# Fourier branch of a diffusion block: one set of channel sums for both mirrored halves, and SiLU as one activation

## The chip, the cores and the metric

One core of a Trainium2 chip runs the whole block. The metric is the device time of one execution in microseconds (us). The program has five engines that work side by side, each through its own instructions in order: TensorE (PE in the profile, with its weight loads as PEld), VectorE (DVE), ScalarE (ACT), GpSimd (POOL) and SyncE (SP, which here only issues transfers).

## The reference, cut to what matters

The block takes 512 tokens of 2048 channels, projects them, and runs two mixers beside each other: attention, and a Fourier mixer over 512 of the projected channels in four groups of 128. The change lies in the Fourier mixer.

```python
def _fourier_mix(u):                      # u: 1 x 512 x 512
    ug = u.astype(jnp.float32).reshape(b, n, N_FNET_GROUPS, FNET_GROUP)
    y = jnp.fft.fftn(ug, axes=(1, 3), norm="ortho").real
    return y.reshape(b, n, FNET_W).astype(u.dtype)

y_b = (_fourier_mix(u_b) * jax.nn.silu(z_b)) @ w_pb
```

For each group, the real part of a 2-D transform over 512 tokens and 128 channels is wanted. With the token sums A (cosine) and B (sine) at frequency f, and the cosine and sine tables C and S over channels, the output is C·A − S·B. A is even in f and B is odd, so at the mirrored frequency 512 − f it is C·A + S·B. The factor of norm="ortho" is 1/256.

## The kernel before, in words

Every product of float32 data is made as three products of a high and a low half (`mm3`, lines 336 to 340): high by high, high by low, low by high. `split_from` (lines 179 to 181) makes the halves: ScalarE rounds the high half (line 180), VectorE subtracts it to get the low half (line 181). So each 1024-column piece of weights costs one instruction on each of those two engines before TensorE can use it (`whi` and `wlo`, or `s` where the halves lie in other slots).

The program starts with the projections of the Fourier branch, then has a short Fourier stage (lines 893 to 968), then goes through the large groups of weights. The Fourier stage works on four groups g:

- `tokens(g)` (line 918) sums over tokens. It makes 12 products on TensorE into two PSUM banks (`pb`), one for even frequencies (258 columns: 129 cosine, 129 sine) and one for odd ones (256 columns). Each bank is split into `ah` and `al`, with even and odd frequencies interleaved.
- `positions(g)` (line 931) sums over channels. It makes 12 products of 256 columns into one bank (`pd`): the lower 256 frequencies from C·A and −S·B (`t` picks a block of `fch`, which holds C, −S and S), and the mirrored 256 from C·A and S·B again, reading `ah` and `al` backwards. The eight products with `ah` come first (line 939), the four with `al` last (line 942). Line 944 on VectorE multiplies the bank by 1/256 and by the gate held in `part`.
- `gate_b(g)` (line 946) turns z into silu(z): ScalarE takes the sigmoid into `e` (line 949), VectorE multiplies (line 950).

The order of calls is tokens 0 and 1, then for each g: gate, positions, the next tokens, and the splits of the first weight pieces of the following product (line 961). TensorE keeps this written order (line 907). On VectorE and ScalarE a scheduler sets the order when the program is built, so a change in one place can move instructions elsewhere.

Behind the stage come the seven products of the first weight group: P1, Q5, P2, Q6, P7, Q3 and Q4, each of four weight pieces. A piece is 12 matmuls of 512 columns. Their results lie in PSUM tiles called `x`, `y` and later `banks`. Some products need sums of the activations (`S`, `Z`, and `ev`, lines 993 and 994), which VectorE makes and splits as well. Weights come in through buffers `wr` and `R`; line 268 adds two pieces, line 276 subtracts them. `qr` and its lines 1208 to 1216 are the norm and rotation of the attention heads. Line 1182 takes sigmoids of the merge gates much later.

Of the kernel before, what the change touches and what calls it, by code (L numbers as in the profile page):

```python
# [10 lines left out]
F32 = mybir.dt.float32  # L11
F32R = mybir.dt.float32r
ACT = mybir.ActivationFunctionType
ALU = mybir.AluOpType
# [4 lines left out]
P = 128  # L19
D = 2048  # L20
T = 512
# [23 lines left out]
RAW = 4  # L45

HL, MORE_HL = 3, 2
EVEN = 258

# [73 lines left out]
def block_kernel(ctx, tc, xT, ctx_rows, ctx_toks, x, c_row, w_ss, w_gate, vecs, qkg, rope, dft_c, dft_s,  # L123
                 w_start, w_g, w_pab, w_o, final_g, out):
    nc = tc.nc
# [30 lines left out]
    def uid(s):  # L156
        cnt[0] += 1
        return f"{s}{cnt[0]}"
# [20 lines left out]
    def split_from(src, hi, lo):  # L179
        first = nc.scalar.activation(hi, src, ACT.Copy)  # L180
        return first, nc.vector.tensor_tensor(lo, src, hi.bitcast(F32), op=ALU.subtract)  # L181
# [16 lines left out]
    def stream(key, src, *a, **k):  # L198
        todo.append(Piece(key, src if isinstance(src, list) else [src], *a, **k))
# [136 lines left out]
    def mm3(o, ah, al, bh, bl, start, stop, cont=False):  # L336

        nc.tensor.matmul(o, ah, bh, start=start, stop=False, skip_group_check=cont)  # L338
        nc.tensor.matmul(o, ah, bl, start=False, stop=False, skip_group_check=cont)  # L339
        nc.tensor.matmul(o, al, bh, start=False, stop=stop, skip_group_check=cont)  # L340
# [25 lines left out]

    for p in start_pieces():
        if p[2:5:2] == (KK - 4, 0):
            stream(("dfts", 0), dft_s[:, : 2 * EVEN], 2 * EVEN, 2, "raw")
            stream(("dftc", 0), dft_c, 3 * P, 1, "raw")  # L370
        elif p[2:5:2] == (KK - 4, 4):
            stream(("dfts", 1), dft_s[:, 2 * EVEN :], T, 2, "raw")
# [71 lines left out]
    q = NGATE  # L444
# [19 lines left out]
    pst, ppool = region("part", "right")  # L464
    part = ppool.tile([P, NS, T], F32, name="part")
# [47 lines left out]
    with tc.issue_after(nc.scalar.activation(ce, cvt, ACT.Exp, scale=-1.0).ins):  # L513
# [6 lines left out]
    fch = ppool.tile([P, 2, 3 * P], F32R, name="fch")  # L520
    fsq = [ppool.tile([P, 2, 2, EVEN], F32R, name="fsq0")]
    rx = pap.tile([P, T], F32, name="rx")
    wacc = bank3()
    def warm(n, src):
# [203 lines left out]
    def split_table(q):  # L728
        split_from(get(("dfts", q)).rearrange("p (a n) -> p a n", a=2), fsq[q][:, 0], fsq[q][:, 1])
# [46 lines left out]
    with tc.manual_schedule(engines={E.PE}):  # L776
# [6 lines left out]
        with tc.manual_schedule(engines={E.Activation, E.DVE}):  # L783
# [25 lines left out]
            for kb in range(1, 4):  # L809
                k = kb + 1  # L810
# [32 lines left out]
            for kb in range(4, KK - 4, 2):  # L843
# [6 lines left out]
                k = kb + 2  # L850
# [45 lines left out]
    fsq.append(fnp.tile([P, 2, 2, 256], F32R, name="fsq1"))  # L896
    split_table(1)

    def halves(a):
# [16 lines left out]
    AH, low = {}, {}  # L916

    def tokens(g):

        ah, al = (fnp.tile([P, 2, 257], F32R, tag=n, bufs=2, name=uid(n)) for n in ("ah", "al"))  # L920
        c = slice(P * g, P * g + P)
        for e in range(2):
            n = fsq[e].shape[-1]
            acc = bank()
            for a in range(2):
                mm3(acc[:, :n], uh[:, a, e, c], ul[:, a, e, c], fsq[e][:, 0, a, :], fsq[e][:, 1, a, :], a == 0, a == 1)
            k = slice(e, 257 - e, 2)
            low[g] = split_from(acc[:, :n].rearrange("p (r f) -> p r f", r=2), ah[:, :, k], al[:, :, k])[1]
        AH[g] = ah, al

    def positions(g):

        ah, al = AH.pop(g)
        acc = bank2()
        steps = [(256 * q, P * (r and 1 + q), (slice(0, 256) if q == 0 else slice(256, 0, -1)), r)
                 for q in range(2) for r in range(2)]
        for n, (o, t, k, r) in enumerate(steps):
            for m, i in enumerate((0, 1)):
                nc.tensor.matmul(acc[:, o : o + 256], fch[:, i, t : t + P], ah[:, r, k], start=n == m == 0, stop=False,
                                 skip_group_check=True)  # L940
        for n, (o, t, k, r) in enumerate(steps):
            nc.tensor.matmul(acc[:, o : o + 256], fch[:, 0, t : t + P], al[:, r, k], start=False, stop=n == 3,
                             skip_group_check=True)
        nc.vector.scalar_tensor_tensor(part[:, 4 + g, :], acc, 1.0 / 256.0, part[:, 4 + g, :], op0=ALU.mult, op1=ALU.mult)

    def gate_b(g):
        z = part[:, 4 + g, :]
        e = fnp.tile([P, T], F32, tag="sil", bufs=1, name=uid("e"))
        nc.scalar.activation(e, z, ACT.Sigmoid)
        nc.vector.tensor_tensor(z, z, e, op=ALU.mult)  # L950

    tokens(0)
    tokens(1)
# [724 lines left out]
    for i in range(NSTEP + 3):  # L1678
        h, t = divmod(i, 4)
# [20 lines left out]
        n = next((n for n, at in enumerate(SUM_AT) if at <= i < at + 3), None)  # L1700
# [19 lines left out]
        if i in GATE_STEPS:  # L1720
            n = NGATE + GATE_STEPS.index(i)
# [91 lines left out]
    o = {}  # L1813
# [255 lines left out]
```

## Time and profile before

| what | us |
|---|---|
| median of three runs | 1290.94 (1290.84 to 1290.96) |
| the profiled execution | 1290.61 |
| its span, first to last instruction | 1288.8 |
| TensorE busy | 1272.9 |
| VectorE busy | 994.7 |
| ScalarE busy | 682.2 |
| GpSimd busy | 170.8 |

The profiled execution's own time is 1.8 us above its span. A timeline row gives the start in us from the span's start, the time of the instruction (or of several alike, with their count), engine, line, operation, output and inputs. What ended an idle time ahead of it stands in brackets. Neighbouring instructions on one engine overlap a little, so the cost of one in a full queue is the distance from its start to the next start, which is called its pitch here.

### The profile page before, as it was taken

The page shows a single profiled execution, that of the slowest core. Times are in us where ns is not written, and L with a number is a line of the kernel's source. Part 1 is how long each engine was busy: PE and PEld are TensorE (multiplying, and loading weights), DVE is VectorE, ACT ScalarE, POOL GpSimd, SP SyncE. Part 2 cuts the span into 40 slices and gives each one's busy share as a digit, 9 for nine tenths or more (in the row PEclk, how much of TensorE's full clock was granted, in tenths as well). Part 3 has the DMA queues.
Part 4 walks back from the last instruction along what each step waited for, and adds up shares of the span by engine and source line. Part 5 has one row for each costly group of instructions (what it writes and reads, how often), then busy time and mean ns, then how long its engine had stood idle before and what let it go on. Part 6 is the DMA issues. An engine that isn't in the chain of part 4 may idle for free.

```text
span 1288.8 us, 17680 instructions
## 1 busy us (share of the span) xinstructions
PE 1272.9 (99%) x6586; PEld 1047.9 (81%) x6586; DVE 994.7 (77%) x1305; ACT 682.2 (53%) x1073; POOL 170.8 (13%) x222
## 2 busy tenths in 40 slices
PE   8999999999999999999999999999999999999997
PEld 5677887888888888888888888888888888888886
DVE  5767899889779787658587666788898777887677
ACT  5322654645556555444355544666667646464544
POOL 0000011111102011012031010012100211211210
PEclk9999999999999999999999999999999999999999
DMA  9998588888988988977879897578852989998986
GB/s 378 408 369 344 208 216 248 237 218 261 227 302 236 301 269 260 291 197 184 278 207 259 286 249 237 182 245 241 270 178 75 249 244 258 244 211 229 225 200 179
DMA packets 104486, 319.14 MB, mean 248 GB/s; under 512 B 9904, under 2 KB 33072, under 8 KB 100432
## 3 DMA queue, kind: packets, MB, share of 16 engines
q1 hardware_dynamic: 55056, 197.40, 42.3%
q0 software_dynamic: 27024, 98.19, 35.6%
q10 hardware_dynamic: 22320, 22.42, 5.1%
q8 instruction: 51, 0.84, 0.3%
q14 instruction: 35, 0.29, 0.1%
HBM read 283.36 MB, written 34.61 MB: 247 GB/s over the span
## 4 chain that ended last, share of the span: by engine, by line
PE 91%; DVE 3%; DMA 2%; ACT 2%; issue 1%; SPq 0%; ACTq 0%; DVEq 0%
PE banks L338 10%; PE banks L339 10%; PE banks L340 10%; PE x L340 9%; PE x L338 9%; PE x L339 9%; PE y L340 7%; PE y L339 7%; PE y L338 7%; PE banks L1543 2%; PE pd L566 2%; PE pb L338 1%; PE pb L339 1%; PE pb L340 1%; PE pc L338 1%; DMA wa<-in_w_ss 1%
## 5 line engine op out<-in xcount | busy, mean ns | idle before, releaser
L180 ACT ACTIVATE whi<-R 128x1024 fp32r<-128x1024 f32 x138 | 145.6, 1060 | 142.1 <-PE banks L340 55.3
L181 DVE TENSOR_TENSOR wlo<-R,whi 128x1024 fp32r<-128x1024 f32 x138 | 167.9, 1222 | 57.9 <-ACT whi L180 57.6
L181 DVE TENSOR_TENSOR wlo<-wr,whi 128x1024 fp32r<-128x1024 f32 (+1 forms) x122 | 147.2, 1214 | 63.1 <-ACT whi L180 63.1
L180 ACT ACTIVATE whi<-wr 128x1024 fp32r<-128x1024 f32 (+1 forms) x122 | 127.4, 1052 | 127.3 <-PE y L340 44.3
L338 PE MATMUL banks<-whi,s 128*128 128x512 f32 (+1 forms) x400 | 157.8, 394 | 0.9 <-DVE ev L1106 0.9
L339 PE MATMUL banks<-wlo,s 128*128 128x512 f32 (+1 forms) x400 | 155.8, 389 | 0.0
L340 PE MATMUL banks<-whi,s 128*128 128x512 f32 (+1 forms) x400 | 155.8, 389 | 0.0
L338 PE MATMUL x<-whi,s 128*128 128x512 f32 x352 | 137.1, 390 | 0.0
L340 PE MATMUL x<-whi,s 128*128 128x512 f32 x352 | 137.0, 389 | 0.0
L339 PE MATMUL x<-wlo,s 128*128 128x512 f32 x352 | 136.9, 389 | 0.0
L338 PE MATMUL y<-whi,s 128*128 128x512 f32 x316 | 123.1, 389 | 0.2 <-DVE cxe L1266 0.2
L339 PE MATMUL y<-wlo,s 128*128 128x512 f32 x316 | 123.1, 390 | 0.0
L340 PE MATMUL y<-whi,s 128*128 128x512 f32 x316 | 122.8, 389 | 0.0
L291 POOL DMA_DIRECT2D R<-in_w_g x64 | 56.0, 875 | 415.2 <-DVE wlo L181 212.6
L180 ACT ACTIVATE s<-wr 128x512 fp32r<-128x512 f32 (+2 forms) x93 | 60.9, 678 | 68.1 <-DMA wr<-cf_d 24.9
L338 PEld LDWEIGHTS banks<-whi,s 128*128 128x128 f32 x400 | 75.2, 188 | 16.6 <-DVE ev L1106 1.3
L181 DVE TENSOR_TENSOR s<-wr,s 128x512 fp32r<-128x512 f32 (+2 forms) x93 | 66.7, 750 | 28.3 <-ACT s L180 27.5
L340 PEld LDWEIGHTS banks<-whi,s 128*128 128x128 f32 x400 | 75.1, 188 | 15.3
L339 PEld LDWEIGHTS banks<-wlo,s 128*128 128x128 f32 x400 | 75.2, 188 | 13.6 <-DVE wlo L181 0.2
L340 PEld LDWEIGHTS x<-whi,s 128*128 128x128 f32 x352 | 66.1, 188 | 13.8
L339 PEld LDWEIGHTS x<-wlo,s 128*128 128x128 f32 x352 | 66.1, 188 | 13.7
L338 PEld LDWEIGHTS x<-whi,s 128*128 128x128 f32 x352 | 66.1, 188 | 13.6
(322 smaller groups left out, 2803.2 us busy)
## 6 DMA issues: line engine op xcount, KB each, us to landing
wr<-in_w_g SPq DMA_DIRECT2D x128, 512.0 KB, 5.8
R<-in_w_g POOLq DMA_DIRECT2D x64, 512.0 KB, 7.3
wa<-in_w_ss SPq DMA_DIRECT2D x31, 1024.0 KB, 9.7
R<-in_w_g SPq DMA_DIRECT2D x32, 512.0 KB, 6.0
wr<-in_w_gate SPq DMA_DIRECT2D x32, 512.0 KB, 5.1
wr<-in_w_o SPq DMA_DIRECT2D x24, 512.0 KB, 7.5
R<-in_w_o POOLq DMA_DIRECT2D x24, 512.0 KB, 9.2
wr<-in_w_pab SPq DMA_DIRECT2D x20, 512.0 KB, 6.0
```

What stands on the lines that cost most here:

```text
L180: first = nc.scalar.activation(hi, src, ACT.Copy)
L181: return first, nc.vector.tensor_tensor(lo, src, hi.bitcast(F32), op=ALU.subtract)
L291: nc.gpsimd.dma_start(chain[e.pc], e.nxt, accum_op=ALU.add)
L338: nc.tensor.matmul(o, ah, bh, start=start, stop=False, skip_group_check=cont)
L339: nc.tensor.matmul(o, ah, bl, start=False, stop=False, skip_group_check=cont)
L340: nc.tensor.matmul(o, al, bh, start=False, stop=stop, skip_group_check=cont)
L566: nc.tensor.matmul(acc[32 * j : 32 * j + 32], c2[:, n, :], w[:, k, :], start=n < 4, stop=n >= KK - 4)
L1543: nc.tensor.transpose(tp[:, k * P : (k + 1) * P], p[:, k * P : (k + 1) * P], ident)
```

## The change

The channel stage makes C·A and S·B once, each as one `mm3` of 258 columns, into two banks (`pd` and `pc`). ScalarE copies the sine bank to `odd` in SBUF. VectorE joins them: a subtraction for 257 frequencies (line 940 of the changed kernel), an addition for the 255 mirrored ones, which reads both inputs backwards (line 941), and a multiplication by the gate (line 942). The factor 1/256 goes into the table `dft_c`, which loses its −S block. Both frequency halves get 129 columns each, so that `ah` and `al` hold 258. The gate is one SiLU activation on ScalarE, in place.

```diff
-        ah, al = (fnp.tile([P, 2, 257], F32R, tag=n, bufs=2, name=uid(n)) for n in ("ah", "al"))
+        ah, al = (fnp.tile([P, 2, FREQ], F32R, tag=n, bufs=2, name=uid(n)) for n in ("ah", "al"))
...
-            k = slice(e, 257 - e, 2)
+            k = slice(e, FREQ, 2)
...
-        acc = bank2()
-        steps = [(256 * q, P * (r and 1 + q), (slice(0, 256) if q == 0 else slice(256, 0, -1)), r)
-                 for q in range(2) for r in range(2)]
-        for n, (o, t, k, r) in enumerate(steps):
-            for m, i in enumerate((0, 1)):
-                nc.tensor.matmul(acc[:, o : o + 256], fch[:, i, t : t + P], ah[:, r, k], start=n == m == 0, stop=False,
-                                 skip_group_check=True)
-        for n, (o, t, k, r) in enumerate(steps):
-            nc.tensor.matmul(acc[:, o : o + 256], fch[:, 0, t : t + P], al[:, r, k], start=False, stop=n == 3,
-                             skip_group_check=True)
-        nc.vector.scalar_tensor_tensor(part[:, 4 + g, :], acc, 1.0 / 256.0, part[:, 4 + g, :], op0=ALU.mult, op1=ALU.mult)
+        acc = [b()[:, :FREQ] for b in (bank2, bank3)]
+        for r, o in enumerate(acc):
+            t = slice(P * r, P * r + P)
+            mm3(o, fch[:, 0, t], fch[:, 1, t], ah[:, r, :], al[:, r, :], True, True)
+        z = part[:, 4 + g, :]
+        y, odd = (fnp.tile([P, n], F32, tag=t, bufs=2, name=uid(t)) for t, n in (("y", T), ("odd", FREQ)))
+        nc.scalar.copy(odd, acc[1])
+        nc.vector.tensor_tensor(y[:, :257], acc[0][:, :257], odd[:, :257], op=ALU.subtract)
+        nc.vector.tensor_tensor(y[:, 257:], acc[0][:, 255:0:-1], odd[:, 255:0:-1], op=ALU.add)
+        nc.vector.tensor_tensor(z, y, z, op=ALU.mult)
...
-        e = fnp.tile([P, T], F32, tag="sil", bufs=1, name=uid("e"))
-        nc.scalar.activation(e, z, ACT.Sigmoid)
-        nc.vector.tensor_tensor(z, z, e, op=ALU.mult)
+        nc.scalar.activation(z, z, ACT.Silu)
...
-    dft_c = np.concatenate([np.cos(a), -np.sin(a), np.sin(a)], axis=1).astype(np.float32)
+    dft_c = (np.concatenate([np.cos(a), np.sin(a)], axis=1) / 256.0).astype(np.float32)
...
-    dft_s = np.concatenate([table(np.arange(0, T // 2 + 1, 2)), table(np.arange(1, T // 2, 2))], axis=1)
+    dft_s = np.concatenate([table(np.arange(e, FREQ, 2)) for e in range(2)], axis=1)
```

The built programs show what stands where. VectorE at the start of the Fourier stage, before: `part` is the gate's storage, `al` the low halves of the token sums (numbers 1440 and 1460 are groups 0 and 1, 1497 is group 2), `wlo` the low half of a weight piece.

```order
L659 TENSOR_TENSOR part<-pc_1425,part 128x512
L950 TENSOR_TENSOR part<-part,e_1516 128x512
L181 TENSOR_TENSOR al_1440<-pb_1441,ah_1439 128x2x129
L181 TENSOR_TENSOR al_1440<-pb_1450,ah_1439 128x2x128
L950 TENSOR_TENSOR part<-part,e_1557 128x512
L181 TENSOR_TENSOR al_1460<-pb_1461,ah_1459 128x2x129
L181 TENSOR_TENSOR al_1460<-pb_1470,ah_1459 128x2x128
L181 TENSOR_TENSOR wlo_1554<-R_1339,whi_1553 128x1024
L944 SCALAR_TENSOR_TENSOR part<-pd_1482,part 128x512
L181 TENSOR_TENSOR al_1497<-pb_1498,ah_1496 128x2x129
L950 TENSOR_TENSOR part<-part,e_1578 128x512
```

VectorE at the same place in the changed program (line numbers there are 4 lower behind the change, and tile numbers differ a little):

```order
L659 TENSOR_TENSOR part<-pc_1425,part 128x512
L181 TENSOR_TENSOR al_1440<-pb_1441,ah_1439 128x258
L181 TENSOR_TENSOR al_1440<-pb_1450,ah_1439 128x258
L181 TENSOR_TENSOR al_1460<-pb_1461,ah_1459 128x258
L181 TENSOR_TENSOR al_1460<-pb_1470,ah_1459 128x258
L181 TENSOR_TENSOR wlo_1550<-R_1339,whi_1549 128x1024
L940 TENSOR_TENSOR y_1488<-pd_1480,odd_1489 128x257
L941 TENSOR_TENSOR y_1488<-pd_1480,odd_1489 128x255
L181 TENSOR_TENSOR al_1495<-pb_1496,ah_1494 128x258
L942 TENSOR_TENSOR part<-y_1488,part 128x512
```

The gate's multiplications no longer stand between the four `al` rows, and line 944's one row is now three. Further on, the second and third `wlo` of the stage stand behind more of the new rows, and other rows change places up to a `wlo` some 60 rows later; from there the order is the old one.

ScalarE at the same place, before: `ah` are the high halves, line 949 the sigmoid, `whi` the high half of a weight piece.

```order
L180 ACTIVATE whi_1595<-R_1341 128x1024
L180 ACTIVATE ah_1439<-pb_1441 128x2x129
L180 ACTIVATE ah_1439<-pb_1450 128x2x128
L949 ACTIVATE e_1557<-part 128x512
L180 ACTIVATE ah_1459<-pb_1461 128x2x129
L180 ACTIVATE ah_1459<-pb_1470 128x2x128
L949 ACTIVATE e_1578<-part 128x512
```

ScalarE there in the changed program, with the SiLU on line 946 and the copy of the sine bank on line 939:

```order
L946 ACTIVATE part<-part 128x512
L180 ACTIVATE whi_1587<-R_1341 128x1024
L180 ACTIVATE ah_1439<-pb_1441 128x258
L946 ACTIVATE part<-part 128x512
L180 ACTIVATE ah_1439<-pb_1450 128x258
L180 ACTIVATE ah_1459<-pb_1461 128x258
L180 ACTIVATE ah_1459<-pb_1470 128x258
L180 ACTIVATE s_286<-wr_1640 128x2x256
L939 COPY odd_1489<-pc_1481 128x258
```

The third gate has moved ahead of `whi`, and the fourth now stands between the two halves of `ah` of group 0.

ScalarE at the first sigmoid of the merge gates, far behind the stage, before:

```order
L180 ACTIVATE s_433<-R_1342 128x2x256
L180 ACTIVATE s_571<-wr_3569 128x2x256
L1182 ACTIVATE ev_3623<-x_3382 128x1024
L180 ACTIVATE s_734<-wr_3569 128x2x256
L1183 DMA g_d<-ev_3623 128x1024
L180 ACTIVATE whi_3670<-wr_3587 128x1024
```

And in the changed program:

```order
L180 ACTIVATE s_433<-R_1342 128x2x256
L180 ACTIVATE s_571<-wr_3561 128x2x256
L1178 ACT_TABLE_LOAD
L1178 ACTIVATE ev_3615<-x_3374 128x1024
L180 ACTIVATE s_734<-wr_3561 128x2x256
L1179 DMA g_d<-ev_3615 128x1024
L180 ACTIVATE whi_3662<-wr_3579 128x1024
```

One more load of ScalarE's function table stands ahead of that sigmoid.

More of the change, by code (lines that the diff above doesn't have):

```diff
@@ L47 @@
 HL, MORE_HL = 3, 2
-EVEN = 258
+FREQ = 258
 FORMS = ("Z5", "S2", "S3", "S4")
@@ L368, in block_kernel @@
         if p[2:5:2] == (KK - 4, 0):
-            stream(("dfts", 0), dft_s[:, : 2 * EVEN], 2 * EVEN, 2, "raw")
-            stream(("dftc", 0), dft_c, 3 * P, 1, "raw")
+            stream(("dfts", 0), dft_s[:, : 2 * FREQ], 2 * FREQ, 2, "raw")
+            stream(("dftc", 0), dft_c, 2 * P, 1, "raw")
         elif p[2:5:2] == (KK - 4, 4):
-            stream(("dfts", 1), dft_s[:, 2 * EVEN :], T, 2, "raw")
+            stream(("dfts", 1), dft_s[:, 2 * FREQ :], 2 * FREQ, 2, "raw")
         stream(("start", p), w_start[p[0] : p[0] + P * p[1]].rearrange("(p c) -> p c", p=P), p[1], p[2 + 1])
@@ L519, in block_kernel @@
                             ce.rearrange("p (j k) -> p j k", j=2), op=ALU.mult)
-    fch = ppool.tile([P, 2, 3 * P], F32R, name="fch")
-    fsq = [ppool.tile([P, 2, 2, EVEN], F32R, name="fsq0")]
+    fch = ppool.tile([P, 2, 2 * P], F32R, name="fch")
+    fsq = [ppool.tile([P, 2, 2, FREQ], F32R, name="fsq0")]
     rx = pap.tile([P, T], F32, name="rx")
@@ L895, in block_kernel @@
     ul = fnp.tile([P, 2, 2, T], F32R, name="ul")
-    fsq.append(fnp.tile([P, 2, 2, 256], F32R, name="fsq1"))
+    fsq.append(fnp.tile([P, 2, 2, FREQ], F32R, name="fsq1"))
     split_table(1)
@@ L918, in tokens @@
     def tokens(g):
-        ah, al = (fnp.tile([P, 2, 257], F32R, tag=n, bufs=2, name=uid(n)) for n in ("ah", "al"))
+        ah, al = (fnp.tile([P, 2, FREQ], F32R, tag=n, bufs=2, name=uid(n)) for n in ("ah", "al"))
         c = slice(P * g, P * g + P)
         for e in range(2):
-            n = fsq[e].shape[-1]
-            acc = bank()
+            acc = bank()[:, :FREQ]
             for a in range(2):
-                mm3(acc[:, :n], uh[:, a, e, c], ul[:, a, e, c], fsq[e][:, 0, a, :], fsq[e][:, 1, a, :], a == 0, a == 1)
-            k = slice(e, 257 - e, 2)
-            low[g] = split_from(acc[:, :n].rearrange("p (r f) -> p r f", r=2), ah[:, :, k], al[:, :, k])[1]
+                mm3(acc, uh[:, a, e, c], ul[:, a, e, c], fsq[e][:, 0, a, :], fsq[e][:, 1, a, :], a == 0, a == 1)
+            k = slice(e, FREQ, 2)
+            low[g] = split_from(acc.rearrange("p (r f) -> p r f", r=2), ah[:, :, k], al[:, :, k])[1]
         AH[g] = ah, al
```

## The prediction

> **What bounds the kernel now.** I read the page first, then the list of waits of TensorE, then the timelines around the Fourier stage, then the busy times by stretch. The page's first part:
>
> ```profile
> PE 1272.9 (99%) x6586; PEld 1047.9 (81%) x6586; DVE 994.7 (77%) x1305; ACT 682.2 (53%) x1073; POOL 170.8 (13%) x222
> ```
>
> TensorE is the bound of the whole: a microsecond taken from it is a microsecond of the total, unless TensorE then has to wait. So the next view is what it waits for from 140 us on (total, times, longest):
>
> ```profile
> PE banks L338 <- DVE ev L1106: 0.9, 1, 0.9
> PE x L339 <- DVE s L181: 0.7, 1, 0.7
> ...
> PE y L340 <- DVE s L181: 0.2, 1, 0.2
> ```
>
> Two of these waits, on low halves from VectorE, come soon behind the changed stage. Here they are on TensorE, and the VectorE rows that end them:
>
> ```profile
> 209.16 0.50 PE L339 MATMUL x<-s,s 128*128 128x512 f32 x1 [0.71 <-DVE s L181]
> 212.64 0.50 PE L340 MATMUL y<-s,s 128*128 128x512 f32 x1 [0.24 <-DVE s L181]
> ```
> ```profile
> 207.81 2.50 DVE L181 TENSOR_TENSOR s<-wr,s 128x512 fp32r<-128x512 f32 x4
> 211.36 1.23 DVE L181 TENSOR_TENSOR s<-S,s 128x1024 fp32r<-128x1024 f32 x1
> ```
>
> Was VectorE late by chance, or full? The busy times by stretch (PE, PEld, DVE, ACT, POOL, granted clock, DMA share, GB/s):
>
> ```profile
> 157.70:212.60 54.90, 53.99 (x236) 43.78 (x234) 54.83 (x67) 29.98 (x48) 10.51 (x13) 1.00 0.82 216
> 212.60:260.00 47.40, 47.36 (x209) 39.23 (x210) 41.29 (x47) 26.99 (x47) 5.64 (x6) 1.00 0.86 260
> ```
>
> From 157.7 to 212.6 VectorE is busy for 54.83 of 54.90 us. It runs without a gap, and TensorE is the one that waits, 0.71 and 0.24 us. So in this stretch VectorE is the bound, although the page's total names TensorE. Behind it VectorE has 6 us to spare in 47. Whatever the change adds to VectorE's queue ahead of 212.6 comes out there on TensorE; whatever it takes from TensorE ahead of 212.6 is waited away.
>
> **The change part by part.** First TensorE:
>
> ```profile
> 150.35 1.13 PE L939 MATMUL pd<-ah,fch 128*128 128x256 f32 x8
> 151.32 0.65 PE L942 MATMUL pd<-al,fch 128*128 128x256 f32 x4
> 151.81 0.28 PE L338 MATMUL pb<-fsq,uh 128*128 128x258 f32 x1
> ...
> 153.24 1.12 PE L939 MATMUL pd<-ah,fch 128*128 128x256 f32 x8
> ...
> 156.13 0.40 PE L338 MATMUL x<-whi,s 128*128 128x512 f32 x1
> ```
>
> Twelve products of positions take 1.46 us (150.35 to 151.81), 0.12 us each; the twelve of tokens, half of them already 258 wide, take 1.43 (151.81 to 153.24). Six products of 258 columns take 0.73, so four groups save 24 × 0.12 = 2.9 us. The two more columns of the odd sums are under 1% of 1.43 and cost nothing that counts.
>
> Now VectorE and ScalarE at the stage:
>
> ```profile
> 145.20 0.69 DVE L659 TENSOR_TENSOR part<-pc,part 128x512 f32<-128x512 f32 x1
> 145.80 0.69 DVE L950 TENSOR_TENSOR part<-part,e 128x512 f32<-128x512 f32 x1
> 146.40 0.76 DVE L181 TENSOR_TENSOR al<-pb,ah 128x258 fp32r<-128x258 f32 x2
> 147.25 0.69 DVE L950 TENSOR_TENSOR part<-part,e 128x512 f32<-128x512 f32 x1
> 147.86 0.75 DVE L181 TENSOR_TENSOR al<-pb,ah 128x258 fp32r<-128x258 f32 x2
> 148.53 1.22 DVE L181 TENSOR_TENSOR wlo<-R,whi 128x1024 fp32r<-128x1024 f32 x1
> 149.66 0.69 DVE L944 SCALAR_TENSOR_TENSOR part<-pd,part 128x512 f32<-128x512 f32 x1
> 150.27 0.43 DVE L181 TENSOR_TENSOR al<-pb,ah 128x258 fp32r<-128x258 f32 x1
> 150.62 0.68 DVE L950 TENSOR_TENSOR part<-part,e 128x512 f32<-128x512 f32 x1
> ...
> 155.96 1.22 DVE L268 TENSOR_TENSOR R<-R,wr 128x1024 f32<-128x1024 f32 x1
> 157.09 0.69 DVE L944 SCALAR_TENSOR_TENSOR part<-pd,part 128x512 f32<-128x512 f32 x1
> 157.69 2.35 DVE L181 TENSOR_TENSOR s<-Z,s 128x1024 fp32r<-128x1024 f32 x2
> ```
> ```profile
> 144.57 1.06 ACT L180 ACTIVATE whi<-R 128x1024 fp32r<-128x1024 f32 x1 [0.41 <-PE pc L339]
> 145.54 0.39 ACT L180 ACTIVATE ah<-pb 128x258 fp32r<-128x258 f32 x1
> 146.24 0.40 ACT L180 ACTIVATE ah<-pb 128x256 fp32r<-128x256 f32 x1 [0.31 <-PE pb L340]
> 146.58 0.64 ACT L949 ACTIVATE e<-part 128x512 f32<-128x512 f32 x1
> 147.12 0.39 ACT L180 ACTIVATE ah<-pb 128x258 fp32r<-128x258 f32 x1
> 147.67 0.42 ACT L180 ACTIVATE ah<-pb 128x256 fp32r<-128x256 f32 x1 [0.16 <-PE pb L340]
> ```
>
> The pitches on VectorE: L950 0.60 (145.80 to 146.40), L944 0.61, one `al` 0.35 (150.27 to 150.62), `wlo` 1.13. New are, per group, an add of 257, an add of 255 and a product of 512. No row of before joins a PSUM and an SBUF operand by an add, but `al` is a subtraction of those very kinds and this size, so 0.34 each; the product is an L950, 0.60. In place of 0.60 + 0.61 = 1.21 stand 1.28. That alone is 4 × 0.07 = 0.3 us more work on VectorE. The backward reading has no VectorE row; the highest bound is the price of a row of twice the size, 0.60 in place of 0.34, so 4 × 0.26 = 1.0 us more. Below 0.33 no row of this size goes, so no gain is taken.
>
> [...]
>
> The second term is where the work falls. The L950 at 145.80 and the one at 147.25 stood in places where VectorE would otherwise have waited for `ah`. They go, and the `al` rows come no sooner, because the fourth gate now stands between ScalarE's two `ah` of group 0. ScalarE, by its pitches: the third gate starts at 144.16, in the 0.41 us that ScalarE idled; `whi` then starts at 144.70 in place of 144.57, the first `ah` at 145.67, the fourth gate at 146.0, the second `ah` at 146.55, the third at 146.95, the fourth at 147.67 as before, since it waits for TensorE. SiLU is not in the trace. I price it as the sigmoid, the row of its size (0.54 from 146.58 to 147.12). The rows of half and double size, `ah` at 0.34 and `whi` at 0.97, bound it: the upper one would widen the holes by some 0.9 us over two gates, the lower narrow them by 0.4. An `al` can start 0.43 us behind the start of its `ah`. So VectorE waits from 145.80 to 146.10, 146.44 to 146.98, 147.32 to 147.38, and 147.72 to 148.10: holes of 1.3 us, which take what the two L950s left (1.2). The first `wlo` starts at 148.45, not 148.53. VectorE has won nothing here.
>
> From the end of that `wlo` to the end of the last gating step, before has 4 × 0.61 + 0.60 + 4 × 0.34 + 2 × 1.13 = 6.66 us of work; in the trace it is 157.69 − 1.13 (the L268 among it) − 149.66 = 6.90. After has 8 × 0.34 + 4 × 0.60 + 4 × 0.34 + 2 × 1.13 = 8.74. That is 1.84 us more, less the 0.08 won: VectorE is 1.8 us behind when it enters its full stretch. Without the 0.24 us of gaps that before had here, the lag against the pitches is 2.1; if the old order's few gaps up to 212.6 close, it is 1.5. I take 1.7.
>
> TensorE meanwhile: with each `positions` shorter, the last one follows its own `tokens` after 0.73 us. Its second product needs the low half, which is done only at 153.6 in this queue, 1.0 us late. So P1 starts at 154.3 in place of 156.13, 1.8 us early and not 2.9.
>
> From there to 212.6 the order differs, but it holds the same set of instructions ahead of the `s<-S` row that TensorE waits for. VectorE had no gap to give, so that row ends 1.7 us later, at 214.3 in place of 212.6. TensorE's 1.8 us turn into waits on the way. What is late next is nothing: behind 212.6 VectorE has spare time, TensorE is the bound again, and it is 1.7 us late for good.
>
> Then the added load of ScalarE's table:
>
> ```profile
> 138.43 1.28 ACT L949 ACT_TABLE_LOAD   x1
> 139.72 0.64 ACT L949 ACTIVATE e<-part 128x512 f32<-128x512 f32 x1
> ```
> ```profile
> 417.98 0.64 ACT L180 ACTIVATE s<-wr 128x512 fp32r<-128x512 f32 x1 [0.82 <-DVE wr L276]
> 419.24 1.03 ACT L1182 ACTIVATE ev<-x 128x1024 f32<-128x1024 f32 x1 [0.63 <-PE x L340]
> 420.17 0.62 ACT L180 ACTIVATE s<-wr 128x512 fp32r<-128x512 f32 x1
> ...
> 421.96 1.06 ACT L180 ACTIVATE whi<-wr 128x1024 fp32r<-128x1024 f32 x1 [1.17 <-PE y L340]
> ```
>
> It takes 1.28 us. ScalarE idles 0.63 ahead of the sigmoid and 1.17 behind the half that follows it, so `whi` at 421.96 is not late. Cost nothing; if the cover were gone, 1.3 us.
>
> The copies of `odd` (258 columns, ScalarE, 0.34 like `ah`), the smaller `fch` table and GpSimd's order have room: ScalarE was busy 29.98 of 54.90 us.
>
> Sum for the profiled execution: 1290.61 + 1.7 = 1292.3. The median lies 0.33 above it, so 1290.94 + 1.7 = **1292.6**, or 0.13% slower. About 0.2% (2.6 us) is what a measurement of this kernel can tell from no change, so this counts as the same.
>
> **The rivals.**
>
> *TensorE's saving comes through.* If VectorE's new order serves TensorE in time up to 212.6, the total falls by 1.8 to 2.9 us, 1288.0 to 1289.1. For it speaks the 99% of the page; against it the 54.83 of 54.90. Chance 0.08, half of it past 0.2%.
>
> *The holes fill.* If the scheduler's order leaves VectorE no holes at 146 to 148, only the 0.3 us of work is left: 1291.2. Against it stands ScalarE's order. Chance 0.12.
>
> *The backward add is slow.* If the 255-column add from PSUM, read backwards, takes 0.60 or more, VectorE's lag is 1.7 + 1.0 = 2.7 and the total 1293.6 or more. It decides from a pitch of 0.56. Against it: TensorE read backwards before, within the x8 rows, at the same 0.12. Chance 0.14.
>
> *The table load is bare.* 1.7 + 1.3: 1293.9. The covers of 0.63 and 1.17 speak against it; chance 0.04. [...]
>
> **How the numbers follow.** The forecast has 0.62. It is the likeliest case, so 1292.6. The range takes in the filled holes below (1291.2, less 0.4 for a faster SiLU) and the slow add above (1293.6, plus 0.4 for the lag of 2.1 in place of 1.7): 1290.8 to 1294.0, leaving out the saving that comes through and the far ends. Faster by over 0.2%: 0.04. Slower: both slow rivals, 0.18. Within: 0.78.
>
> **What would show it.** Right: VectorE idle about 1.3 us between 145.8 and 148.5; the adds at 0.34; P1 at about 154.3; VectorE without a gap from there to about 214; waits of TensorE of some 5.5 us in all up to 214 (0.95 + 2.9 + 1.7), 1.0 of them inside `positions`, where 0.95 stood; no wait near 420. Wrong: TensorE at the first product behind 212.6 earlier than before, an add far from 0.34, or a difference that arises behind 260 us.

## The result, and the profile after

The changed kernel takes 1294.2 us (median of 12 runs, 1293.4 to 1297.1) against 1291.0 (12 runs, 1290.7 to 1292.1). The ratio is 1.0024, with a 95% interval of 1.0017 to 1.0032: 3.2 us slower, 1.6 us more than forecast. The profiled execution takes 1293.8 us with a span of 1292.0, 3.2 us more than before.

The page of the changed kernel, engines and chain:

```profile
PE 1270.5 (98%) x6562; PEld 1044.4 (81%) x6562; DVE 994.5 (77%) x1309; ACT 683.7 (53%) x1078; POOL 171.0 (13%) x222
...
PE 90%; DVE 5%; DMA 2%; ACT 2%; issue 1%; POOL 0%; SPq 0%; ACTq 0%; DVEq 0%
```

TensorE has 24 matmuls fewer, and VectorE's part of the chain has grown. Where, the table by stage says (columns: length, then busy time of PE, PEld, DVE, ACT and POOL with counts, clock, DMA share, GB/s):

```profile
157.70:212.60 54.90, 52.06 (x226) 41.76 (x225) 54.15 (x66) 30.75 (x48) 9.93 (x12) 1.00 0.79 206
212.60:260.00 47.40, 46.71 (x206) 38.34 (x205) 42.33 (x47) 27.41 (x47) 6.19 (x7) 1.00 0.91 266
```

In the first stretch TensorE now does 2.8 us less than there is time, and VectorE, full before, has a gap of 0.75. VectorE's timeline through the Fourier stage and behind it:

```profile
144.94 0.69 DVE L659 TENSOR_TENSOR part<-pc,part 128x512 f32<-128x512 f32 x1
145.78 0.43 DVE L181 TENSOR_TENSOR al<-pb,ah 128x258 fp32r<-128x258 f32 x1 [0.16 <-ACT ah L180]
146.60 0.43 DVE L181 TENSOR_TENSOR al<-pb,ah 128x258 fp32r<-128x258 f32 x1 [0.40 <-ACT ah L180]
147.20 0.43 DVE L181 TENSOR_TENSOR al<-pb,ah 128x258 fp32r<-128x258 f32 x1 [0.17 <-ACT ah L180]
147.92 0.43 DVE L181 TENSOR_TENSOR al<-pb,ah 128x258 fp32r<-128x258 f32 x1 [0.29 <-ACT ah L180]
148.26 1.22 DVE L181 TENSOR_TENSOR wlo<-R,whi 128x1024 fp32r<-128x1024 f32 x1
149.39 0.42 DVE L940 TENSOR_TENSOR y<-pd,odd 128x257 f32<-128x257 f32 x1
149.73 0.41 DVE L941 TENSOR_TENSOR y<-pd,odd 128x255 f32<-128x255 f32 x1
150.06 0.42 DVE L181 TENSOR_TENSOR al<-pb,ah 128x258 fp32r<-128x258 f32 x1
150.39 0.68 DVE L942 TENSOR_TENSOR part<-y,part 128x512 f32<-128x512 f32 x1
150.99 0.42 DVE L181 TENSOR_TENSOR al<-pb,ah 128x258 fp32r<-128x258 f32 x1
...
157.44 0.69 DVE L942 TENSOR_TENSOR part<-y,part 128x512 f32<-128x512 f32 x1
158.05 2.36 DVE L268 TENSOR_TENSOR R<-R,wr 128x1024 f32<-128x1024 f32 x2
...
166.84 1.23 DVE L181 TENSOR_TENSOR wlo<-R,whi 128x1024 fp32r<-128x1024 f32 x1 [0.75 <-ACT whi L180]
...
213.52 1.23 DVE L181 TENSOR_TENSOR s<-S,s 128x1024 fp32r<-128x1024 f32 x1
```

The brackets ahead of the `al` rows sum to 1.02 us. A bracket reads less than the wait costs here: a row's start, less the start of the row ahead of it and that row's pitch (0.60 for L659, 0.34 for an `al`), gives 0.24, 0.48, 0.26 and 0.38, together 1.36 us. Both adds cost 0.33 to 0.34. The last row is the low half of S for which TensorE waits. It started at 211.36 before, so it is 2.16 us later. The hole at 166.84 was not foreseen. ScalarE shows what made it:

```profile
160.56 1.07 ACT L180 ACTIVATE whi<-R 128x1024 fp32r<-128x1024 f32 x1 [0.71 <-PE x L340]
163.76 1.16 ACT L180 ACTIVATE s<-wr 128x512 fp32r<-128x512 f32 x2 [2.13 <-DMA wr<-in_w_g]
164.81 1.05 ACT L180 ACTIVATE s<-S 128x1024 fp32r<-128x1024 f32 x1
165.76 1.04 ACT L180 ACTIVATE whi<-R 128x1024 fp32r<-128x1024 f32 x1
```

ScalarE stands for 2.13 us before a weight load, and the `whi` that VectorE needs is two rows behind it in ScalarE's order. In the profile before, the same `s<-wr` came at 160.68, 3.08 us earlier. The load's buffer comes free when VectorE's L268 has read it, and that row, at 155.96 before, is at 158.05 now, behind the last product of the join. That is 2.09 of the 3.08 us; the load itself also took longer to land, 4.4 us in place of 3.5. So VectorE's lag came back to it through a load and through ScalarE. TensorE's timeline at its waits:

```profile
152.31 0.34 PE L338 MATMUL pd<-ah,fch 128*128 128x258 f32 x1
153.40 0.39 PE L339 MATMUL pd<-al,fch 128*128 128x258 f32 x1 [0.75 <-DVE al L181]
...
153.99 0.28 PE L340 MATMUL pc<-ah,fch 128*128 128x258 f32 x1
154.78 0.50 PE L338 MATMUL x<-whi,s 128*128 128x512 f32 x1 [0.51 <-ACT odd L939]
...
206.12 0.50 PE L339 MATMUL x<-wlo,s 128*128 128x512 f32 x1 [1.34 <-DVE wlo L181]
...
210.54 0.50 PE L338 MATMUL x<-s,s 128*128 128x512 f32 x1 [1.44 <-ACT s L180]
...
214.80 0.50 PE L340 MATMUL y<-s,s 128*128 128x512 f32 x1 [0.69 <-DVE s L181]
```

P1 starts at 154.78, 1.35 us earlier than before. The matmul that waits for the low half starts at 214.80 in place of 212.64: 2.16 us later. The order of TensorE is the same in both from there on, so each matmul can be set against its twin. The twins are 1.6 to 2.25 us apart up to 1124 us; there it becomes 3.2, where TensorE waits for `s<-yb_d`, a fetch of stored sums that did not make it wait before (line waited for: us in total, times, longest):

```profile
PE banks L1653 <- DMA s<-yb_d: 0.9, 1, 0.9
```

Between the second profiles of the two kernels the twins are 1.7 to 2.0 apart up to there and 2.5 behind it.

### The profile page after: what moved, and what is told of

Read it like the earlier page. It is cut to its first block, busy times and chain, and to the rows that moved or that the text cites. A ratio compares the mean times of both kernels' runs of the same rounds, so it can differ in the third digit from the quotient of the medians.

```text
span 1292.0 us, 17637 instructions
## 1 busy us (share of the span) xinstructions
PE 1270.5 (98%) x6562; PEld 1044.4 (81%) x6562; DVE 994.5 (77%) x1309; ACT 683.7 (53%) x1078; POOL 171.0 (13%) x222
## 4 chain that ended last, share of the span: by engine, by line
PE 90%; DVE 5%; DMA 2%; ACT 2%; issue 1%; POOL 0%; SPq 0%; ACTq 0%; DVEq 0%
PE banks L338 10%; PE banks L339 10%; PE banks L340 10%; PE x L339 8%; PE x L340 8%; PE x L338 8%; PE y L340 7%; PE y L339 7%; PE y L338 7%; PE banks L1539 2%; PE pd L566 2%; PE pb L338 1%; PE pb L339 1%; PE pc L338 1%; PE pb L340 1%; PE pc L339 1%
```

## The experiments

Fourteen kernels were run. The columns are the median, the ratio to the kernel before with its 95% interval, the start of the awaited low half of S on VectorE, and how long the fetch of `s<-yb_d` took from issue to landing, both in the profiled execution.

| kernel | median us | ratio (interval) | low half of S | fetch |
|---|---|---|---|---|
| before, with its second profile | 1290.8 to 1291.3 | 1 | 211.36, 211.85 | 8.7, 8.6 |
| changed, with its second profile | 1294.2 | 1.0024 (1.0017 to 1.0032) | 213.52, 213.79 | 10.0, 9.7 |
| silu_only | 1289.6 | 0.9989 (0.9980 to 0.9998) | 210.46 | 8.8 |
| fourier_only | 1294.1 | 1.0023 (1.0014 to 1.0032) | 214.21 | 10.0 |
| pool_product | 1292.9 | 1.0017 (1.0008 to 1.0026) | 213.31 | 9.2 |
| pe_twice | 1294.4 | 1.0026 (1.0016 to 1.0037) | 213.69 | 8.6 |
| sums_first | 1292.5 | 1.0012 (1.0003 to 1.0021) | 212.87 | 9.9 |
| silu_spare | 1292.2 | 1.0011 (1.0002 to 1.0020) | 212.90 | 8.8 |
| pool_twice | 1293.3 | 1.0025 (1.0014 to 1.0036) | 213.88 | 9.4 |
| no_product | 1290.5 | 0.9996 (0.9987 to 1.0005) | 210.39 | 10.2 |
| before_shift | 1293.5 | 1.0022 (1.0013 to 1.0031) | 211.33 | 9.0 |
| after_shift | 1296.1 | 1.0036 (1.0023 to 1.0049) | 213.88 | 10.0 |
| after_fetch | 1295.4 | 1.0031 (1.0019 to 1.0043) | 216.82 | 9.1 |
| before_fetch | 1311.2 | 1.0157 (1.0144 to 1.0171) | 230.62 | 9.7 |

Two executions of one kernel put the low half up to 0.5 us apart, so smaller differences there say nothing. The last two kernels start later as a whole, by 3 and by 19 us.

**The two halves of the change.** SiLU alone, on the kernel before:

```diff
-        e = fnp.tile([P, T], F32, tag="sil", bufs=1, name=uid("e"))
-        nc.scalar.activation(e, z, ACT.Sigmoid)
-        nc.vector.tensor_tensor(z, z, e, op=ALU.mult)
+        nc.scalar.activation(z, z, ACT.Silu)
```

> The kernel before with one edit: silu of z by one SiLU activation, the old cosine and sine sums kept. VectorE loses four products of 0.60 us (2.4 us) in the stage where it is full. Theory (VectorE's work up to the awaited split of S sets the stage): TensorE's waits of 0.71 and 0.24 us at 209 to 213 us shrink or go, so 0.4 to 0.95 us faster than before, about 1290.2 us. Rival A (the holes that SiLU leaves at 146 to 148 us are the cost): no gain, or up to 1 us slower. Rival B (the extra table load at 419 us is paid): 0.3 to 0.9 us slower than before, with a wait of TensorE near 420 us.

1289.6 us, 1.35 us faster (0.3 to 2.6 by the interval). Of TensorE's waits in the stage one is left:

```profile
PE y L340 <- DVE s L181: 0.2, 1, 0.2
```

The theory held, with a somewhat larger gain than it gave. This is the version that beats both kernels. The other half, the changed kernel with these lines put back:

> The changed kernel with the old gate (sigmoid and a product on VectorE). VectorE then has four joins of two adds (0.34 each) and a product (0.60) in place of one step of 0.61 per group: 2.7 us more than before, without the holes that SiLU left. Theory: the work passes into the total, less 0.2 to 0.5 us of gaps: 2.2 to 2.7 us slower than before if the load for s_571 is in time, up to 3.5 with the hole behind it; so 1293.2 to 1294.5 us, about the changed kernel's time or up to 0.5 us above. Rival A (SiLU's holes or its table load make the loss): within 0.5 us of before plus 2.7 less 1.3, at most 1292.4. Rival C (the 0.9 us wait for s<-yb_d at 1124 us was one execution's chance): no wait there in this profile.

1294.05 us, 3.1 slower than before. VectorE has no holes at 146 to 148 us, but 0.87 of idle time at 167.53 for the same late load, and `s<-yb_d` is late as well. So rivals A and C fell. SiLU's 2.4 us of VectorE time, worth 1.35 us alone, are worth nothing in the changed kernel by the medians: 1294.2 with it, 1294.05 without. In the profiles the awaited row does come 0.4 to 0.7 us later without it, about what two executions of one kernel differ by.

**Does TensorE's time count?** The changed kernel with each sum of `positions` made twice:

```diff
-            mm3(o, fch[:, 0, t], fch[:, 1, t], ah[:, r, :], al[:, r, :], True, True)
+            for _ in range(2):
+                mm3(o, fch[:, 0, t], fch[:, 1, t], ah[:, r, :], al[:, r, :], True, True)
```

> The changed kernel with each cosine and sine sum of positions made twice over: 24 matmuls of 0.12 us more, 2.9 us, as many as the change took away; the outputs are unchanged. Theory (TensorE only waits in this stage): within 0.5 us of the changed kernel, TensorE's waits up to 214 us smaller by 2 to 3 us. Rival E (TensorE is the bound and VectorE's rows are only late because TensorE's order shifted): 2.9 us slower than the changed kernel, near 1297 us.

1294.4 us, only 0.2 above the changed kernel, but not in the way that the theory gave, so that the number is partly luck. TensorE's waits up to 214 us are 4.2 us by the brackets, against 4.7 in the changed kernel: 0.5 less and not 2 to 3. VectorE's low half of S stands within 0.2 us of where it was, but TensorE now waits ahead of it, 2.09 and 1.60 us, for other low halves. A stretch at half clock follows (below), which costs about 1.4 us in seven matmuls. At 230 us TensorE is 2.45 us behind its twins of the changed kernel. It gets 0.7 back on the way to 1122 us, about what two executions of one kernel differ by there, and 1.1 at 1124, where it does not wait for `s<-yb_d`. So this run does not settle what TensorE's 2.9 us are worth. That they were waited away in the changed kernel stands on its own trace, where TensorE waits 4.7 us in the place of 0.95.

**Is it VectorE's work, or its holes?** The kernel with SiLU alone, and a spare product whose result goes nowhere:

```diff
         nc.vector.scalar_tensor_tensor(part[:, 4 + g, :], acc, ...)
+        spare = fnp.tile([P, T], F32, tag="spare", bufs=2, name=uid("spare"))
+        nc.vector.tensor_tensor(spare, part[:, 4 + g, :], part[:, 4 + g, :], op=ALU.mult)
```

> The kernel before with SiLU and a spare product of 512 columns on VectorE behind each gating step: VectorE has as many operations and as much work as before, but four products of 0.60 us stand behind the first wlo instead of in the gaps at 145 to 148 us. The spare results go nowhere; the outputs are unchanged. Theory (holes that the sigmoid products filled are the greater part of the changed kernel's loss): 1.0 to 1.5 us slower than before, plus up to 0.8 if the load for s_571 comes late too, 1292.0 to 1293.3. Rival (the joins' own work and order make the loss): within 0.4 us of before.

1292.2 us, 1.25 slower than before (0.3 to 2.6 by the interval; the profiled executions are 0.9 apart), with the same amount of VectorE work. Of the gates' four products three stood ahead of the first `wlo` before (140.39, 145.80, 147.25); all four spare ones stand behind it. The expectation puts four into the gaps at 145 to 148, but only two stood there. So work that is moved out of gaps, with none added, costs about as much as the term that the prediction named (1.2).

**The late load.** The sums R + wr are written ahead of the last product (`sum_piece` is the loop of line 268, made once):

```diff
+        if g == 3:
+            for e in ahead[3:5]:
+                if e.kind != "raw":
+                    sum_piece(e)
         nc.vector.tensor_tensor(z, y, z, op=ALU.mult)
```

> The changed kernel with the next pieces' sums R + wr on VectorE written ahead of the last group's product, so that the first of them leaves VectorE one product and one low half earlier (about 1.7 us) and the load of the weights behind it, s_571, starts as much earlier. Theory (the hole of 0.75 us at 166 us on VectorE is a late load in front of ScalarE's next halves): the hole goes and the awaited split of S comes 0.5 to 0.8 us sooner, so 0.5 to 0.8 us faster than the changed kernel, 1293.3 to 1293.7. Rival (the hole is covered by what VectorE would wait for anyway): within 0.2 us of the changed kernel.

VectorE has no idle time between 149 us and the awaited row, which starts at 212.87, 0.65 or 0.92 us earlier than in the two profiles of the changed kernel. So the hole was real and its cause is shown. The medians stand 1.7 us apart, more than the 0.5 to 0.8 expected, but the profiled executions only 0.5 (1293.34 against 1293.8; the second profile of the changed kernel took 1293.37). What of the 1.7 lies beyond the hole is not resolved.

**Relief for VectorE.** The product goes to GpSimd:

```diff
-        nc.vector.tensor_tensor(z, y, z, op=ALU.mult)
+        nc.gpsimd.tensor_tensor(z, y, z, op=ALU.mult)
```

> The changed kernel with the last product of each join (y times z) on GpSimd. VectorE loses 2.4 us against the changed kernel and has 2.1 us less than before. Theory: the lag at the awaited split goes, and part of TensorE's 2.9 us comes through: 2.2 to 4.5 us faster than the changed kernel, 1289.5 to 1292.0 us. Rival B (table load, bank of the first product behind the last odd copy, or anything behind 260 us): less than 1 us faster than the changed kernel. Rival D (GpSimd in the way of its own DMA issues): TensorE waits for R or wr, slower than 1293 us.

1292.9 us, 1.3 faster than the changed kernel: too little for the theory, and neither rival names the reason. At 230 us TensorE is only 0.2 ahead of its twins in the changed kernel; 0.5 more come between 600 and 1122 us, where two executions of one kernel differ by as much, and 0.8 at 1124, where this kernel does not wait for `s<-yb_d`. So hardly any of the gain arises in the stage. VectorE's rows, then GpSimd's:

```profile
151.87 0.43 DVE L181 TENSOR_TENSOR al<-pb,ah 128x258 fp32r<-128x258 f32 x1
152.22 2.20 DVE L181 TENSOR_TENSOR wlo<-R,whi 128x1024 fp32r<-128x1024 f32 x1
...
155.34 1.21 DVE L181 TENSOR_TENSOR wlo<-R,whi 128x1024 fp32r<-128x1024 f32 x1
...
157.13 3.87 DVE L268 TENSOR_TENSOR R<-R,wr 128x1024 f32<-128x1024 f32 x2
```

```profile
150.79 2.54 POOL L942 TENSOR_TENSOR part<-y,part 128x512 f32<-128x512 f32 x2 [71.26 <-PE pc L340]
153.63 0.58 POOL L962 DMA_DIRECT2D b_d<-part  x1 [0.30 <-POOL part L942]
155.57 4.35 POOL L942 TENSOR_TENSOR part<-y,part 128x512 f32<-128x512 f32 x2 [1.36 <-DVE y L941]
```

Beside GpSimd's products a `wlo` takes 2.20 us in place of 1.22 and two L268 take 3.87 in place of 2.36. That is 2.5 us more, and eats the 2.4 that VectorE was to gain; the `al` row at 151.87, one of whose inputs lies in PSUM, takes its usual 0.43. A `wlo` that had begun at 155.34, just ahead of GpSimd's second pair, took 1.21. The trace shows the times, not what held these rows up. In the table by stretches of 3.4 us the same run shows a second loss:

```profile
152.60:156.00 3.40, 1.25 (x8) 0.85 (x7) 3.40 (x5) 0.62 (x2) 1.74 (x3) 1.00 0.39 155
156.00:159.40 3.40, 3.22 (x8) 2.55 (x9) 3.40 (x5) 2.98 (x4) 3.40 (x2) 0.50 0.01 4
159.40:162.80 3.40, 3.40 (x16) 2.80 (x15) 3.40 (x3) 2.06 (x3) 1.11 (x2) 1.00 0.83 243
```

Where TensorE had worked for 1.25 us of 3.40, it was granted half its clock in the next 3.40: 8 matmuls in place of 16. To test that, the wait was filled with the second set of sums as above:

> The kernel with the product on GpSimd, with each cosine and sine sum made twice over on TensorE (24 matmuls of 0.12 us, 2.9 us more; outputs unchanged). In the run with the product on GpSimd TensorE was granted 0.50 of its clock from 156.0 to 159.4 us, behind a wait of 1.82 us, and lost 1.6 us in eight matmuls. Theory (too little work in a stretch of 3.4 us takes the clock down): with the wait filled by matmuls the clock stays at 1.00 and the time is no more than 0.5 us longer than without them, or up to 1.6 us shorter. Rival (the slow matmuls come from GpSimd's or a DMA's traffic): the slow stretch stays and the time grows by 1 to 2.9 us.

The same two stretches:

```profile
152.60:156.00 3.40, 3.10 (x24) 2.72 (x23) 3.40 (x6) 1.96 (x5) 1.50 (x2) 1.00 0.51 154
156.00:159.40 3.40, 2.89 (x17) 2.38 (x16) 3.40 (x6) 2.69 (x5) 2.08 (x4) 1.00 0.38 154
```

The stretch from 156.0 to 159.4 is at clock 1.00, and 24 matmuls more cost 0.5 us instead of 2.9. The theory held.

**Without the product.** The sum is stored without the gate z; one multiplication per group is left out:

```diff
...
-        nc.vector.tensor_tensor(y[:, :257], acc[0][:, :257], odd[:, :257], op=ALU.subtract)
-        nc.vector.tensor_tensor(y[:, 257:], acc[0][:, 255:0:-1], odd[:, 255:0:-1], op=ALU.add)
-        nc.vector.tensor_tensor(z, y, z, op=ALU.mult)
+        nc.vector.tensor_tensor(z[:, :257], acc[0][:, :257], odd[:, :257], op=ALU.subtract)
+        nc.vector.tensor_tensor(z[:, 257:], acc[0][:, 255:0:-1], odd[:, 255:0:-1], op=ALU.add)
```

> The changed kernel without the product of the join: the sum of the Fourier branch is stored without the gate z, which leaves one multiplication per group out of the computation. VectorE has 2.4 us less than the changed kernel and 2.1 us less than before, and GpSimd takes nothing over. Theory (VectorE's room alone decides whether TensorE's 2.9 us come through): 0.95 us of old waits go, 2.9 us come through less 0.5 for the bank behind the last odd copy and up to 0.8 for a late low half: 2.5 us faster than before, 1287.6 to 1289.3 us. Rival (the bank behind odd, the table load, or what comes behind 260 us holds the loss): 1290.5 us or more.

1290.5 us, no faster than before: the theory missed, and the time is the rival's. VectorE still idles 1.29 us by the brackets ahead of the `al` rows and starts the low half of S only 0.97 earlier. Against its twins in the kernel before TensorE is 1.0 us early at 212.6, 1.6 at 672, 1.8 at 1122, and 0.5 behind 1124, where this wait took back 1.3 (1.1 by the bracket):

```profile
PE banks L1652 <- DMA s<-yb_d: 1.1, 1, 1.1
```

**The fetch at 1124 us.** To know whether it was chance, both kernels were profiled again:

> The changed kernel once more, as it is. Theory (the wait of 0.9 us for s<-yb_d at 1124 us comes of where the changed kernel's transfers fall against each other): the wait is there again, 0.7 to 1.0 us. Rival (chance of one execution): no wait, or under 0.3 us.

> The kernel before once more, as it is. Both theories: no wait for s<-yb_d, the fetch issued near 1114.8 lands in 8.6 to 8.8 us; chance of one execution would show as 9.5 us or more.

The wait was there again in the changed kernel (0.6 us, just under the 0.7 to 1.0 expected; the fetch 9.7) and not in the one before (8.6). Next, both with eight matmuls more in the middle of the program, where `made` counts the calls of `mm3`:

```diff
+        made[0] += 1
+        if made[0] > 1000 and start and bh.shape[-1] == 512 and not cont:
+            made[0] = -10000
+            for _ in range(8):
+                nc.tensor.matmul(o, ah, bh, start=True, stop=False, skip_group_check=True)
```

> The kernel before with eight matmuls of 512 columns, 1.8 us, made once more on TensorE in the middle of the program (overwritten by the sum that follows; outputs unchanged). Everything behind them comes 1.8 us later, as in the changed kernel, but nothing else differs. Theory (how long the fetch of s<-yb_d takes hangs on when it is issued: 8.6 to 8.8 us from 1113.5 to 1115.7, 9.2 to 10.0 from 1116.1 to 1117.0, 8.6 at 1118.65): the fetch issued near 1116.6 takes 9.5 to 10 us, TensorE waits 0.4 to 0.9 us for it, and the time is 2.2 to 2.7 us longer than before. Rival (the changed kernel's own order of transfers makes it late): 8.7 us, no wait, 1.6 to 1.8 us longer than before.

> The changed kernel with the same eight matmuls, 1.8 us, in the middle of the program (outputs unchanged). Theory (the moment of issue decides): the fetch of s<-yb_d is issued near 1118.7 and takes 8.6 us, TensorE does not wait for it, and the time grows by 0.9 to 1.2 us only. Rival (its own order decides): the wait of 0.6 to 0.9 us stays and the time grows by 1.6 to 1.8 us.

The moment of issue does not decide: issued at 1116.25, before's fetch took 9.0 us and nobody waited; issued at 1120.23, the changed kernel's took 10.0. The changed kernel grew by 1.9 us, about what the rival gave. The kernel before grew by 2.7, which is the theory's number, but not by the theory's wait: TensorE waited 0.8 us for a `wlo` instead. But the tables of transfers showed a line that went with the late landings. It is the queue that brings instructions; here one microsecond of the changed kernel, five behind the issue of the fetch (queue: packets, MB, share):

```profile
q0 software_dynamic: 30, 0.12, 61.9%
q1 hardware_dynamic: 32, 0.13, 36.3%
q8 instruction: 1, 0.02, 5.5%
```

Over the whole program this queue brings 51 packets and 0.84 MB, 16 KB each. TensorE has 6562 matmuls and as many weight loads, 257 of its rows to a packet. I take these to be its instructions, one block about every 25 us; the two tests below bear it out. The change took 48 rows away, so every later block comes later against the program, and one that came 0.8 and 2.4 us before the issue of `s<-yb_d` in the two profiles of before comes 5.1 and 5.2 us behind it in those of the changed kernel, while its transfer runs. Two kernels tested it, moving only where the blocks fall, by tiny matmuls at the start. The changed kernel with 24 more:

```diff
         warm(8, ones)
+        warm(12, ones[:, :8])
```

> The changed kernel with twelve more tiny warm-up matmuls (8 columns) while TensorE waits at 5 us: 24 more matmuls and 24 more weight loads in its queue, as many as the change took out, at a place that costs nothing. Theory (TensorE's instructions are fetched in blocks of 16 KB, 256 instructions; 48 fewer move each later block by some 5.5 us against the program, and one now falls into the fetch of s<-yb_d): the block's fetch moves back to before the transfer, which lands in 8.6 to 9.0 us in place of 9.7 to 10.0, the wait at 1124 us goes, and the time falls by 0.5 to 0.9 us below the changed kernel. Rival (the transfer is late for another reason): it lands in 9.7 us or more, and the wait of 0.6 to 0.9 us stays.

The kernel before with 104 more, 48 rows short of a block:

```diff
-        warm(8, ones)
+        warm(60, ones[:, :8])
```

> The kernel before with 60 tiny warm-up matmuls in place of 8 of 128 columns at the start: 208 more entries in TensorE's queue, which is 48 short of a block of 256, so that its blocks stand against the program as in the changed kernel. Theory: the fetch of s<-yb_d has a block of instructions in its midst, lands in 9.7 to 10.2 us, TensorE waits 0.6 to 1.1 us for it, and the time is 0.5 to 1.1 us longer than before. Rival (the changed kernel's order or memory makes the transfer late): 8.6 to 9.0 us, no wait, the same time as before within 0.3 us.

The tiny matmuls were dearer than I had reckoned and put the whole program back, by 3 us and by 19, so the medians (1295.4 and 1311.2, ratios 1.0031 (1.0019 to 1.0043) and 1.0157 (1.0144 to 1.0171)) don't answer the question; the place does. The changed kernel with them, at the fetch (the rows of one line, and the time from issue to landing):

```profile
L1640 POOL DMA_DIRECT2D s<-yb_d x1: 850/850/850, 1120.3 to 1120.3; - x1
...
DMA to landing us min/median/max: 9.1/9.1/9.1
```

The kernel before with them, the same view, with who waited for it:

```profile
L1643 POOL DMA_DIRECT2D s<-yb_d x1: 850/850/850, 1133.5 to 1133.5; - x1
...
  PE banks L1657: 0.6, 1
...
DMA to landing us min/median/max: 9.7/9.7/9.7
```

In the first the block comes 1.2 us before the issue, TensorE does not wait, and its distance from the changed kernel falls from 3.4 to 2.55 us right there. In the second the block comes 5.2 us behind the issue, the wait appears, and the distance from the kernel before grows by 0.8. The theory held both ways, though the first landing (9.1) is just above the 8.6 to 9.0 expected: the late fetch goes with the block of instructions, not with the order or the tables of the changed kernel. Over all sixteen profiles, the seven with the block 5.0 to 5.3 us behind the issue land in 9.7 to 10.2 us, and one with it 5.7 behind in 9.2. Those with it ahead of the issue land in 8.6 to 9.1, save pool_twice with 9.4, for which I have no reason. With another fetch of `yb_d` the same comparison gives less: the one issued near 1025 us took 10.1 to 10.8 with a block 6 to 8 us behind its issue, and 9.5 to 10.5 without.

## Why the prediction was wrong, step by step

- *TensorE's saving is waited away.* Right for the changed kernel, by its trace; pe_twice, which was to test it, does not settle it. The low half of group 3 cost 0.97 by the starts (153.40 against 152.31 of the matmul ahead, less 0.12), as forecast. A wait that I had not seen stands at P1, whose bank is the one that the last `odd` copy reads: 0.51 by the bracket, 0.67 by the starts. So P1 starts at 154.78, not 154.3.
- *Adds 0.34, product 0.60.* Right, backwards too: 0.34 and 0.33. That rival falls.
- *SiLU as the sigmoid, and holes of 1.3.* Right. SiLU's pitch is 0.53 and 0.55, and the holes are 1.36 us by the starts. The first `wlo` starts at 148.26, forecast 148.45, but the whole stage began 0.26 earlier (L659 at 144.94, before 145.20). Between the second profiles it began 0.19 later, so I take that for the chance of one execution. silu_spare shows that this displaced work alone costs about 1.25.
- *"VectorE had no gap to give, so that row ends 1.7 us later."* This step failed: the row is 2.16 later (1.94 between the second profiles). Up to the last gating step the sum was right: from L659 to the end of that step VectorE takes 1.75 us more than before (158.05 − 144.94, against 157.69 − 1.13 − 145.20), forecast 1.84 − 0.08. The early start made that a lag of 1.49 in this execution, where 1.7 was taken. Behind it VectorE did have a gap, the hole at 166.84: 0.75 by the bracket, 0.85 by the starts. With it the row would be 2.34 later; what took back the other 0.18 I have not traced. I argued from the set of instructions ahead of the row, but a set keeps its length only if its inputs come in time. The load for the `s<-wr` rows hung on L268, one of the rows that I let slip.
- *"What is late next is nothing … it is 1.7 us late for good."* This step failed outright. Behind 260 us TensorE lost another 1.0 (0.6 between the second profiles), at the fetch whose lateness goes with the instruction blocks that taking 48 rows out of its queue moved. The prediction listed a difference behind 260 us as what would prove it wrong. Its two failures, 0.5 and 1.0, make up the distance between forecast and result.
- *The table load costs nothing.* Right. It stands on ScalarE as forecast, and the `whi` behind it waits for TensorE, not TensorE for it:

```profile
420.83 1.28 ACT L1178 ACT_TABLE_LOAD   x1
422.12 1.03 ACT L1178 ACTIVATE ev<-x 128x1024 f32<-128x1024 f32 x1
423.05 0.62 ACT L180 ACTIVATE s<-wr 128x512 fp32r<-128x512 f32 x1
...
424.16 1.06 ACT L180 ACTIVATE whi<-wr 128x1024 fp32r<-128x1024 f32 x1 [0.50 <-PE y L340]
```

- *Waits of 5.5 us up to 214.* They sum to 4.7 by the brackets, and to 5.7 by the starts, each less the start of the matmul ahead and its usual distance (0.12, or 0.23 for 512 columns).

What stays open: why one packet of 16 KB goes with a delay of about 1.2 us in this fetch of 512 KB and with less in another, what TensorE's 2.9 us would be worth if VectorE kept up, and how much of the 1.7 us between sums_first and the changed kernel is the hole.

## What to carry to other kernels

When an engine is full in a stage, ask not only how much work a change gives it but which loads hang on the rows that slip: a freed buffer, a load and another engine's order can bring the lag back as a new hole, here one of 0.75 us. A change with two halves is worth measuring by halves; here the one (SiLU) gains 1.35 us alone and nothing that the medians show with the other. And where some tenths of a per cent count, a late difference far from the edit can come from where blocks of instructions fall: here 48 rows fewer in TensorE's queue moved such a block from 0.8 us ahead of the issue of a fetch to 5.1 us behind it, and the fetch took 10.0 us in place of 8.7.

## What the runs showed of the hardware that I had not expected

- What I take to be a block of TensorE's instructions, 16 KB about every 25 us, comes in over a DMA queue of its own while the data moves. In a busy stretch a 512 KB fetch with such a block 5.0 to 5.3 us behind its issue took 9.7 to 10.2 us, and 8.6 to 9.4 with the block ahead of it.
- In pool_product TensorE was granted 0.50 of its clock for 3.4 us behind 3.4 us in which it had worked for 1.25. In pe_twice it was 0.51 behind 0.73 us of work, and from there its matmuls stood 0.43 us apart in place of 0.23. Behind 2.06 us of work in 3.41 (the changed kernel, 203.06 to 206.47) it kept its clock, 1.00 in the next 3.41 us. The two stretches of pe_twice:

```profile
209.70:213.10 3.40, 0.73 (x2) 0.30 (x2) 3.40 (x6) 1.16 (x3) 1.43 (x2) 1.00 0.24 40
213.10:216.50 3.40, 3.28 (x8) 2.60 (x9) 2.94 (x4) 0.74 (x2) 0.00 (x0) 0.51 0.98 228
```

- Beside GpSimd's products of two SBUF tiles in pool_product, a `wlo` of VectorE, which has two SBUF inputs, took 2.20 us in place of 1.22, and an `al`, which has one input in PSUM, took its usual 0.43.
